# Gathering the experts of 32 more tokens, and building the expert weights from factored one-hots

## The chip, the cores and the metric

The kernel runs on one core of a Trainium2 chip. The metric is the device time of one execution in microseconds (us); three runs of the kernel before gave 1546.71 (median), from 1545.36 to 1548.38. Durations and waits below come from one profiled execution of 1544.91 us.

## The reference

One decoder layer for 512 tokens of width 1024: an input projection, differential attention and retention side by side, an output projection, then the PEER experts, then a gated input embedding and a last RMSNorm. The change is in the experts alone:

```python
qry = (m @ w_query).reshape(B, S, 8, 2, 128)
scores = jnp.einsum('bshcd,hckd->bshck', qry, sub_keys)
vals, idx = lax.top_k(scores, 16)                    # 16 of 128 keys, for each half
cand = vals[..., 0, :, None] + vals[..., 1, None, :]
cand_idx = idx[..., 0, :, None] * 128 + idx[..., 1, None, :]
top_s, top_pos = lax.top_k(cand.reshape(..., 256), 16)
expert = take_along_axis(cand_idx, top_pos)          # i * 128 + j
gates = softmax(top_s)
act = gelu(einsum('cd,ced->ce', x, u[expert])) * gates
out = einsum('ce,ced->cd', act, v[expert])
```

Each token has 8 x 16 = 128 chosen experts out of 16,384. `u` and `v` are 16,384 x 1024 in float32.

## The kernel before

The experts are computed in two ways. For the first ND = 384 tokens (three blocks of 128) all experts are computed densely and weighted with a matrix that is zero where an expert wasn't chosen. For the last 128 tokens (block 3) the chosen rows of `u` and `v` are gathered. To keep float32 precision each dense product is a sum of three matmuls of high and low parts (`wh`, `wl`, `ah`, `al`, `xh`, `xl`): ScalarE cuts the high part (L746, L755), VectorE subtracts to get the low one (L762, L764).

**Dense units.** 128 `u` units (L769, by `project` and `product3` at L85): for 128 experts i * 128 + j with the same i, 24 matmuls that stream the 384 tokens into the PSUM tile `ps`; ScalarE applies Gelu into `av` (L810). 128 `v` units (L782): 18 matmuls that add the 128 weighted experts, with the tokens as the stationary operand (three blocks of 128) and 512 columns of `v`, into the PSUM tiles `acc`. A unit's table tile of 512 KB is loaded into `wraw` three to four units ahead (RAW = 4) on SyncE's queue. The first 24 units (KEEP) keep `av` in SBUF; those of the early loop after them store it to the DRAM tile `a` and load it again.

**Gathered tokens.** GpSimd issues an indirect DMA (L848) that fetches, for each of 128 tokens, the row of one rank r out of `u` or `v` (512 KB). `sparse_step` (L853) consumes it on VectorE: for `u` a dot product with `mtok` into a column of `act` (L859), for `v` a multiply-add into `yacc` (L861). There are 256 such steps, in the list `order` (from L826). Three row buffers (ROWS) stand in `late`; six more (MORE) exist from the start of the late loop until shortly before the point END (64 units before its end), where the loads for the last stage begin. A buffer that comes free is refilled by `gather` (L836).

**Weights.** `choose(b)` (L1006) ranks the candidates of a block on VectorE; for blocks 0 to 2 a `turn` puts i, j and gate into columns by token (`it`, `jt`, `mh`, `ml`: the gate in two float16 parts). `weights_map(b, z)` (L1111) takes a RUN of 32 tokens, eight at a time: four VectorE instructions over 1024 elements (L1163 to L1166) make one-hots of j (`A`) and of i times the two gate parts (`Bh`, `Bl`), and `tail` (L1117) multiplies them on TensorE, 16 matmuls for eight tokens, into `pg`, which ScalarE copies out; the map of a RUN is written to `g_d` and read back as `gv` in quads for the `v` units (L752 multiplies it into `av`).

**Order.** Everything is issued in an order that the program works out from written costs. In the early loop (L1190) each turn is one `u` unit; it adds 4.1 to a clock `pe` (and 0.5 for a tail) and 1.25 to a clock `dve`, and then takes steps of the generator `side` (choose(3), then for each of the three blocks choose and four RUNs) for as long as `dve` is behind `pe`; each step adds 0.86 (SLOW) times the cost that it yields. After each group of eight tokens up to two gather steps are taken if a third clock, of DMA traffic, allows them (L1169). The loop ends when `side` is exhausted. What it leaves, the late loop (L1379) does: the remaining `u` units and all 128 `v` units, eight tiles of the gate weight, the remaining gather steps spread so that planned traffic per unit is level (`level`, L1376) up to the last twelve units, and the loads that the end needs (`ends`, L1353).

The lines that set the pace of the planner:

```python
clock["dve"] += 1.25                       # L1194, one u unit's wl
clock["pe"] += 4.1                         # L1201, one u unit
clock["dve"] += SLOW * c                   # L1225, c is what a step yields: 2.75 for a token group
while done[0] < n_sp and (traffic + LOAD <= level * passed or n >= total - SPARSE_END):   # L1407
```

Of the kernel before, what the change touches and what calls it, by code (L numbers as in the profile page):

```python
# [23 lines left out]
F32 = mybir.dt.float32  # L24
# [3 lines left out]
I32 = mybir.dt.int32  # L28
# [11 lines left out]
NT = 3  # L40
ND = NT * P
HEADS = 8
# [12 lines left out]
def block_kernel(ctx: ExitStack, tc, t):  # L55
# [89 lines left out]
    with pool("wa", 2, side="right") as wa, pool("sm", 2, side="right") as sm, \  # L145
# [552 lines left out]
        g_sp = late.tile([P, P], F32, name="g_sp")  # L698
        act = late.tile([P, P], F32, name="act")
        junk = late.tile([P, D], BF16, name="junk")  # L700
        nc.gpsimd.memset(yacc, 0.0)
# [34 lines left out]
        def prepare(u, low):  # L736
            kind, i = u
            w = raw.pop(u)
            if kind == "g":
                for d in range(2):  # L740
                    c = slice(d * S, (d + 1) * S)
                    scaled_split(fin["gh"][i][d], fin["gl"][:, i, c], w[:, c], gains[:, G_PLE, i:i + 1])
                return
            wh = wt.tile([P, D], F32R, name="wh", tag="wh")
            wl = wt.tile([P, D], F32R, name="wl", tag="wl")
            nc.scalar.activation(wh, w, AF.Copy)  # L746
            parts[u] = wh, wl
            if kind == "v":
                gv, av = inputs.pop(u)
                if gv is not None:  # L750
                    av3 = av.rearrange("p (z t) -> p z t", t=RUN)
                    nc.vector.tensor_tensor(av3, gv, av3, op=OP.mult)  # L752
                ah = vp[0].tile([P, ND], F32R, name="ah", tag="ah", bufs=2)
                al = vp[0].tile([P, ND], F32R, name="al", tag="al", bufs=2)
                nc.scalar.activation(ah, av, AF.Copy)  # L755
                parts[u] += ah, al
            if low is nc.gpsimd:

                nc.scalar.activation(wl, w, AF.Copy, scale=-1.0)
                nc.gpsimd.dma_start(wl.bitcast(F32), w, accum_op=OP.add)  # L760
            else:
                low.tensor_tensor(wl, w, wh.bitcast(F32), op=OP.subtract)  # L762
            if kind == "v":
                nc.vector.tensor_tensor(al, av, ah.bitcast(F32), op=OP.subtract)  # L764

# [53 lines left out]

        vp, acc, count, done_u = [], [], [0], []  # L820
        writes, spills = [], []
# [14 lines left out]
        def gather():  # L836

            while due:
                more = due.pop(0)
                if issued[0] >= n_sp or (more and not extra):  # L840
                    continue
                n = issued[0]
                issued[0] += 1
                table, r = order[n]
# [3 lines left out]
                nc.gpsimd.indirect_dma_start(out=rows[n], out_offset=None, in_=t[table],  # L848
                                             in_offset=bass.IndirectOffsetOnAxis(ap=e_sp[:, r:r + 1], axis=0))

        at_more, MORE = {}, 6

        def sparse_step():  # L853
            n = done[0]
            done[0] += 1
            table, r = order[n]
            row = rows.pop(n)
            if table == "peer_u":
                nc.vector.tensor_tensor_reduce(junk, row, mtok, 1.0, 0.0, OP.mult, OP.add, act[:, r:r + 1])  # L859
            else:  # L860
                nc.vector.scalar_tensor_tensor(yacc, row, act[:, r:r + 1], yacc, op0=OP.mult, op1=OP.add)  # L861
            due.append(at_more.pop(n))
            if table == "peer_u" and r % TOPK == TOPK - 1:
                hs = slice(r + 1 - TOPK, r + 1)
                nc.scalar.activation(act[:, hs], act[:, hs], AF.Gelu)
                nc.vector.tensor_tensor(act[:, hs], act[:, hs], g_sp[:, hs], op=OP.mult)

        with pool("wp", 2, side="right") as wpp:
# [50 lines left out]
            nc.sync.dma_start(ple_d[:, :, halves[1]], kp)  # L919
            nc.vector.tensor_tensor(mtok, mn[3], gffn, op=OP.mult)  # L920
    k_stack = ctx.enter_context(ExitStack())
    g_stack = ctx.enter_context(ExitStack())
    with pool("pk") as pk, pool("psG", 2, space=PSUM) as psG, pool("psT", space=PSUM) as psT:
# [73 lines left out]
        gsp = g_stack.enter_context(pool("gsp", side="right"))  # L997
        mh = pk.tile([P, ND], F16, name="mh")
        ml = pk.tile([P, ND], F16, name="ml")
        it = pk.tile([P, ND], BF16, name="it")  # L1000
        jt = pk.tile([P, ND], BF16, name="jt")
        later, soon = [], []
# [3 lines left out]
        def choose(b):  # L1006
# [77 lines left out]
            if b >= NT:  # L1084
                nc.vector.scalar_tensor_tensor(ij[:, 0], ij[:, 0], float(NKEY), ij[:, 1], op0=OP.mult, op1=OP.add)
                nc.vector.tensor_copy(e_sp, ij[:, 0].rearrange("p h k -> p (h k)"))
                due.extend([False] * ROWS)
                yield 0.5
                return
            turned = []  # L1090

            def turn():

                bs = slice(b * P, (b + 1) * P)
# [4 lines left out]
                nc.scalar.activation(it[:, bs], pt[:, 0], AF.Copy)  # L1099
# [11 lines left out]
        def weights_map(b, z):  # L1111
# [31 lines left out]
            def write(q0, q1):  # L1143
                nc.sync.dma_start(g_d[q0:q1, :, g].rearrange("q j x t -> j q (x t)"),
                                  gs[0][:, q0 * QUAD:q1 * QUAD].rearrange("j (q x) t -> j q (x t)", x=QUAD))

            for t0 in range(0, RUN, 8):
                while len(later) >= LATER:
# [9 lines left out]
                def per_token(x):  # L1158
                    c = b * P + z * RUN + t0
# [80 lines left out]
    def open_fin():  # L1240
# [9 lines left out]
        fin["gl"] = fp.tile([P, KC, D], F32R, name="gl", bufs=1)  # L1250
        for name in ("gate_b", "final_gain"):
            fin[name] = fp.tile([P, D], F32, name=name, bufs=1)
        fin["st"] = fp.tile([P, 8], F32, name="st", bufs=1)
# [66 lines left out]
    with pool("acc", space=PSUM) as pa:  # L1320
        vp.append(mp)
        acc += [[pa.tile([P, S], F32, name=f"acc{b}{d}") for d in range(2)] for b in range(NT)]
        V_END, total_u = 24, 0
# [54 lines left out]
        for n, u in enumerate(seq):  # L1378
# [32 lines left out]
            if 0 <= n - end_at < len(ends):  # L1411
                name, b = ends[n - end_at]
                if b is None:
                    nc.sync.dma_start(fin[name], row_src(name))
                else:
                    nc.sync.dma_start(fin[name][:, b], sources[name][:, b])
# [96 lines left out]
```

## Time and profile before

| | |
|---|---|
| median of three runs | 1546.71 us |
| profiled execution | 1544.91 us |
| its span, first to last instruction | 1543.1 us |
| TensorE busy | 1515.5 us (98%) |
| VectorE busy | 1223.0 us (79%) |
| ScalarE busy | 676.4 us (44%) |
| GpSimd busy | 384.1 us (25%) |
| moved by DMA | 401.67 MB |

The time is that of the execution; the span leaves out 1.8 us around the first and the last instruction. Busy time counts an engine as busy if any of its instructions runs, so a share is an average over stages with different limits, and a busy TensorE need not run at its peak. A line named L85 is a helper: the tile names (`ps`, `S`, `wo`) tell its callers apart.

### The profile page before, as it was taken

How to read it: one execution, taken by the hardware profiler on the slowest of the kernel's cores; microseconds unless marked ns; L12 is line 12 of the kernel's file. 1: busy time of each engine (PE TensorE's matmuls, PEld its weight loads, DVE VectorE, ACT ScalarE, POOL GpSimd, SP SyncE). 2: the span in 40 equal slices, each digit the busy share in tenths (PEclk: the TensorE clock that was granted, in tenths of full speed). 3: DMA queues.
4: the chain of work that ended last, by engine and by line, in shares of the span. 5: the costliest groups of instructions: out<-in, count | busy, mean ns of one | idle time of the engine just before them, and what ended most of it. 6: DMA issues, size and time to landing. Idle time of an engine off the chain costs nothing.

```text
span 1543.1 us, 22928 instructions
## 1 busy us (share of the span) xinstructions
PE 1515.5 (98%) x8197; PEld 1342.0 (87%) x8197; DVE 1223.0 (79%) x2529; ACT 676.4 (44%) x1075; POOL 384.1 (25%) x321
## 2 busy tenths in 40 slices
PE   8999999999999999999999999999999999999996
PEld 6787887888999999999999989898988888888885
DVE  3767555779998999898985888988888885987755
ACT  4554645444634454453434333333333333453444
POOL 1300000110023203202224555554434311422000
PEclk9999999999999999999999999999999999999999
DMA  6412335773468979887999989999999988999601
GB/s 230 148 62 80 103 107 205 215 189 110 161 205 276 299 239 306 303 287 251 308 312 372 382 315 377 343 377 393 365 355 368 348 323 314 352 377 354 243 17 41
DMA packets 163378, 401.67 MB, mean 260 GB/s; under 512 B 14687, under 2 KB 77418, under 8 KB 163136
## 3 DMA queue, kind: packets, MB, share of 16 engines
q1 hardware_dynamic: 123248, 256.06, 46.7%
q0 software_dynamic: 40016, 144.15, 27.6%
q8 instruction: 64, 1.05, 0.3%
q14 instruction: 50, 0.41, 0.1%
HBM read 350.61 MB, written 42.21 MB: 255 GB/s over the span
## 4 chain that ended last, share of the span: by engine, by line
PE 88%; DVE 7%; DMA 3%; ACT 1%; issue 1%; SPq 0%; ACTq 0%; DVEq 0%
PE ps L85 44%; PE acc L782 31%; PE S L85 2%; PE S L322 2%; PE ps L518 1%; PE pg L1123 1%; PE pg L1125 1%; PE wo L85 1%; DVE wl L762 1%; PE sc L957 1%; DMA wraw<-in_w_val_dram 1%; DMA av<-a 1%; PE po L458 1%; PE po L639 1%; DMA wraw<-in_gate_w_dram 1%
## 5 line engine op out<-in xcount | busy, mean ns | idle before, releaser
L85 PE MATMUL ps<-xh,wh 128*128 128x384 f32 (+1 forms) x1312 | 464.0, 354 | 1.6 <-ACT av L810 0.8
L85 PE MATMUL ps<-xh,wl 128*128 128x384 f32 (+1 forms) x1312 | 457.3, 349 | 3.4 <-DVE wl L762 3.4
L85 PE MATMUL ps<-xl,wh 128*128 128x384 f32 (+1 forms) x1320 | 457.9, 347 | 0.0
L762 DVE TENSOR_TENSOR wl<-wraw,wh 128x1024 fp32r<-128x1024 f32 x260 | 317.4, 1221 | 77.5 <-ACT wh L746 76.8
L746 ACT ACTIVATE wh<-wraw 128x1024 fp32r<-128x1024 f32 x272 | 286.7, 1054 | 201.2 <-PE ps L85 94.7
L848 POOL DMA_INDIRECT row<-in_peer_u_dram,e_sp x128 | 174.0, 1359 | 360.6 <-DVE yacc L861 225.4
L848 POOL DMA_INDIRECT row<-in_peer_v_dram,e_sp x128 | 169.6, 1325 | 374.2 <-DVE act L859 277.3
L85 PEld LDWEIGHTS ps<-xh,wl 128*128 128x128 f32 x1312 | 247.4, 189 | 15.7 <-DVE wl L762 4.1
L85 PEld LDWEIGHTS ps<-xh,wh 128*128 128x128 f32 x1312 | 247.9, 189 | 13.9 <-ACT av L810 1.1
L85 PEld LDWEIGHTS ps<-xl,wh 128*128 128x128 f32 x1320 | 249.2, 189 | 10.2
L782 PE MATMUL acc<-wh,ah 128*128 128x512 f32 x768 | 237.1, 390 | 0.6 <-ACT ah L755 0.6
L782 PE MATMUL acc<-wl,ah 128*128 128x512 f32 x768 | 236.8, 390 | 0.0
L782 PE MATMUL acc<-wh,al 128*128 128x512 f32 x768 | 236.7, 390 | 0.0
L782 PEld LDWEIGHTS acc<-wl,ah 128*128 128x128 f32 x768 | 144.2, 188 | 30.1
L782 PEld LDWEIGHTS acc<-wh,al 128*128 128x128 f32 x768 | 144.2, 188 | 30.0 <-DVE al L764 0.2
L782 PEld LDWEIGHTS acc<-wh,ah 128*128 128x128 f32 x768 | 144.0, 188 | 30.1 <-ACT ah L755 1.0
L861 DVE SCALAR_TENSOR_TENSOR yacc<-row,act,yacc 128x1024 f32<-128x1024 f32 x128 | 163.9, 1280 | 2.0 <-DMA row<-in_peer_v_dram,e_sp 1.8
L859 DVE CUSTOM_DVE_ANT_0 junk<-row,mtok 128x1024 bf16<-128x1024 f32 x128 | 156.0, 1219 | 1.9 <-DMA row<-in_peer_u_dram,e_sp 1.6
L755 ACT ACTIVATE ah<-av 128x384 fp32r<-128x384 f32 x104 | 54.6, 525 | 228.5 <-PE acc L782 179.3
L764 DVE TENSOR_TENSOR al<-av,ah 128x384 fp32r<-128x384 f32 x104 | 57.8, 556 | 63.0 <-ACT ah L755 62.8
L1133 ACT ACTIVATE gs<-pg 128x832 f32<-128x832 f32 x48 | 41.6, 866 | 144.8 <-PE pg L1125 144.8
L752 DVE TENSOR_TENSOR av<-gv,av 128x384 f32<-128x384 f32 x104 | 57.5, 553 | 7.4 <-DMA av<-a 6.8
(288 smaller groups left out, 1686.4 us busy)
## 6 DMA issues: line engine op xcount, KB each, us to landing
wraw<-in_u_t_dram SPq DMA_DIRECT2D x128, 512.0 KB, 5.8
wraw<-in_peer_v_dram SPq DMA_DIRECT2D x128, 512.0 KB, 6.8
gv<-g_d SPq DMA_DIRECT2D x26, 768.0 KB, 8.4
a<-av SPq DMA_DIRECT2D x72, 192.0 KB, 4.2
g_d<-gs SPq DMA_DIRECT2D x24, 576.0 KB, 7.4
av<-a SPq DMA_DIRECT2D x72, 192.0 KB, 6.1
wraw<-in_w_in_t_dram SPq DMA_DIRECT2D x16, 512.0 KB, 3.3
wraw<-in_wq_t_dram SPq DMA_DIRECT2D x16, 512.0 KB, 4.1
```

The source lines that it names most:

```text
L85: nc.tensor.matmul(out, a, b, start=first and k == 0, stop=last and k == n - 1)
L322: nc.tensor.matmul(out, *((a, b) if q_first else (b, a)), start=n == 0, stop=n == 1)
L746: nc.scalar.activation(wh, w, AF.Copy)
L752: nc.vector.tensor_tensor(av3, gv, av3, op=OP.mult)
L755: nc.scalar.activation(ah, av, AF.Copy)
L762: low.tensor_tensor(wl, w, wh.bitcast(F32), op=OP.subtract)
L764: nc.vector.tensor_tensor(al, av, ah.bitcast(F32), op=OP.subtract)
L782: nc.tensor.matmul(acc[b][d], a[:, c], bb[:, d * S:(d + 1) * S], start=f, stop=l)
L848: nc.gpsimd.indirect_dma_start(out=rows[n], out_offset=None, in_=t[table], in_offset=bass.IndirectOffsetOnAxis(ap=e_sp[:, r:r + 1], axis=0))
L859: nc.vector.tensor_tensor_reduce(junk, row, mtok, 1.0, 0.0, OP.mult, OP.add, act[:, r:r + 1])
L861: nc.vector.scalar_tensor_tensor(yacc, row, act[:, r:r + 1], yacc, op0=OP.mult, op1=OP.add)
L1133: nc.scalar.activation(gs[0][:, :, t0:t0 + 8], pgi[:, KEEP:], AF.Copy, scale=2.0 ** -15)
```

## The change

Of block 2 only the first 96 tokens stay dense: ND is 352 (11 RUNs), and the last 32 tokens of that block are gathered like block 3. For them a tile `e_x` holds the experts with partitions (q, x): 32 tokens x in each of four groups q of 32 ranks, so that one indirect DMA of 128 rows serves four ranks of each of the 32 tokens. That is 32 more steps for each table, 64 in all, with their own tokens `mtok_x`, gates `g_x`, activations `act_x` and sum `yacc_x`, listed in `order` behind the 256 of before. At the end `fold`, a matrix of ones and zeros, adds the four groups of `yacc_x` into the last 32 tokens of `acc` of block 2 by two float32 matmuls. `u` units stream 352 columns; for the `v` units `ah` and `al` lie in three rotating pairs of 384 columns whose last 32 are zeroed once.

The one-hot of i times a gate part, before one comparison and two products over 1024 elements for eight tokens, is now made of a one-hot of the high part of i (`ih`, 16 wide, times each gate part: `hh`, `hl`) and one of its rest (`il`, 8 wide: `lo`), built for 32 tokens at once; for eight tokens two products over 1024 elements give `Bh` and `Bl`. `turn` has four more small instructions that split i. A RUN now yields 1.5 + 4 x 2.05 in place of 4 x 2.75. `gate_b` and `final_gain` are loaded into `mtok_x` and `mtok` at `total - 8` rather than into tiles of their own with `ends`.

```diff
+NX = 32
+ND = NT * P - NX
+QX = P // NX
...
-                ah = vp[0].tile([P, ND], F32R, name="ah", tag="ah", bufs=2)
-                al = vp[0].tile([P, ND], F32R, name="al", tag="al", bufs=2)
-                nc.scalar.activation(ah, av, AF.Copy)
+                ah, al = pads[0]
+                pads.append(pads.pop(0))
+                nc.scalar.activation(ah[:, :ND], av, AF.Copy)
...
-        for h in range(HEADS + 1):
-            for k in range(TOPK):
-                if h < HEADS:
-                    order.append(("peer_u", h * TOPK + k))
-                if h > 0:
-                    order.append(("peer_v", (h - 1) * TOPK + k))
+        for x, n in ((0, P // TOPK), (1, NX // TOPK)):
+            for h in range(n + 1):
+                for k in range(TOPK):
+                    if h < n:
+                        order.append(("peer_u", x, h * TOPK + k))
+                    if h > 0:
+                        order.append(("peer_v", x, (h - 1) * TOPK + k))
...
+            nc.vector.tensor_tensor(mn[2], mn[2], gffn, op=OP.mult)
+            for q in range(QX):
+                nc.gpsimd.dma_start(mtok_x[q * NX:(q + 1) * NX], mn[2][P - NX:])
...
+            if b == NT - 1:
+                ef = pk.tile([P, HEADS, TOPK], F32, name="ts", tag="ts")
+                ei = pk.tile([P, P], I32, name="pos", tag="pos")
+                nc.vector.scalar_tensor_tensor(ef, ij[:, 0], float(NKEY), ij[:, 1], op0=OP.mult, op1=OP.add)
+                nc.vector.tensor_copy(ei, ef.rearrange("p h k -> p (h k)"))
+                gx = ij[:, 2].rearrange("p h k -> p (h k)")
+                for q in range(QX):
+                    for x, y in ((e_x, ei), (g_x, gx)):
+                        nc.gpsimd.dma_start(x[q * NX:(q + 1) * NX], y[P - NX:, q * NX:(q + 1) * NX])
+                yield 0.5
...
+                step8 = 1.5 * 2.0 ** 26
+                nc.vector.tensor_scalar(gb, ih, -3.5, step8, op0=OP.add, op1=OP.add)
+                nc.vector.tensor_scalar(gb, gb, -step8, None, op0=OP.add)
+                nc.vector.tensor_tensor(il, ih, gb, op=OP.subtract)
+                nc.vector.tensor_copy(ih, gb)
...
+            nc.vector.tensor_tensor(hl, io2[:, 0:P:8][:, None].to_broadcast(parts_of), per_pair(ih, P // 8), op=OP.is_equal)
+            nc.vector.tensor_tensor(lo, io2[:, 0:8][:, None].to_broadcast([P, RUN // 2, 8, 2]), per_pair(il, 8), op=OP.is_equal)
+            nc.vector.tensor_tensor(hh, hl, per_pair(mh, P // 8), op=OP.mult)
+            nc.vector.tensor_tensor(hl, hl, per_pair(ml, P // 8), op=OP.mult)
+            yield 1.5
...
-                nc.vector.tensor_tensor(Bl, io, per_token(it), op=OP.is_equal)
                 nc.vector.tensor_tensor(A, io, per_token(jt), op=OP.is_equal)
-                nc.vector.tensor_tensor(Bh, Bl, per_token(mh), op=OP.mult)
-                nc.vector.tensor_tensor(Bl, Bl, per_token(ml), op=OP.mult)
+                g4, full = slice(t0 // 2, t0 // 2 + 4), [P, 4, P // 8, 8, 2]
+                for x, y in ((Bh, hh), (Bl, hl)):
+                    nc.vector.tensor_tensor(x.rearrange("p g (h l) k -> p g h l k", l=8), y[:, g4, :, None].to_broadcast(full),
+                                            lo[:, g4, None].to_broadcast(full), op=OP.mult)
-                yield 2.75
+                yield 2.05
...
-                for z in range(P // RUN):
+                for z in range((min(ND, b * P + P) - b * P) // RUN):
...
-        ends = [("hs", b) for b in (3, 0, 1, 2)] + [("final_gain", None), ("gate_b", None)]
+        ends = [("hs", b) for b in (3, 0, 1, 2)]
...
             if n == total - 8:
                 assert done[0] == n_sp
                 add_experts(3, [yacc[:, d * S:(d + 1) * S] for d in range(2)])
+                for d in range(2):
+                    nc.tensor.matmul(acc[NT - 1][d], fold, yacc_x[0][:, d * S:(d + 1) * S], start=False, stop=False)
+                for name in ("final_gain", "gate_b"):
+                    nc.sync.dma_start(fin[name], row_src(name))
```

## Rows read from the trace of the kernel before

**Rows 1.** Page, the chain that ended last: shares by engine, then by line.

```profile
PE 88%; DVE 7%; DMA 3%; ACT 1%; issue 1%; SPq 0%; ACTq 0%; DVEq 0%
PE ps L85 44%; PE acc L782 31%; PE S L85 2%; PE S L322 2%; PE ps L518 1%; PE pg L1123 1%; PE pg L1125 1%; PE wo L85 1%; DVE wl L762 1%; PE sc L957 1%; DMA wraw<-in_w_val_dram 1%; DMA av<-a 1%; PE po L458 1%; PE po L639 1%; DMA wraw<-in_gate_w_dram 1%
```

**Rows 2.** Busy us by stage: its length, engines with instructions, granted clock, DMA share, GB/s.

```profile
261.00:368.00 107.00, 105.37 (x532) 88.28 (x531) 81.27 (x479) 50.72 (x68) 10.45 (x12) 1.00 0.67 178
368.00:430.00 62.00, 56.67 (x316) 55.61 (x314) 61.17 (x272) 33.85 (x41) 3.06 (x3) 0.97 0.39 134
430.00:826.00 396.00, 395.18 (x2767) 387.53 (x2768) 348.06 (x643) 174.00 (x265) 90.68 (x70) 1.00 0.85 282
826.00:1435.00 609.00, 608.44 (x2863) 526.37 (x2863) 511.85 (x660) 232.04 (x322) 249.84 (x184) 1.00 0.96 358
1435.00:1484.00 49.00, 49.00 (x221) 40.60 (x220) 29.64 (x47) 19.07 (x28) 0.00 (x0) 1.00 0.40 141
```

**Rows 3.** Chain in order of time: start us, us, what (xcount of instructions).

```profile
359.15 0.91 PE sc L957 x8
...
430.75 9.69 PE ps L85 x48
440.44 0.07 PE pg L1123
...
441.36 8.38 PE ps L85 x48
...
809.80 33.33 PE ps L85 x192
...
1097.64 57.16 PE acc L782 x252
```

**Rows 4.** VectorE's instructions in order of time: start us, us, instruction.

```profile
455.21 0.69 DVE L1163 TENSOR_TENSOR Bl<-io,it 128x1024 f16<-128x1024 bf16 x1
...
457.75 1.22 DVE L762 TENSOR_TENSOR wl<-wraw,wh 128x1024 fp32r<-128x1024 f32 x1
458.88 0.17 DVE L800 TENSOR_TENSOR kept<-kept,av 128x16 f32<-128x16 f32 x1
458.97 1.22 DVE L859 CUSTOM_DVE_ANT_0 junk<-row,mtok 128x1024 bf16<-128x1024 f32 x1
...
460.23 1.23 DVE L859 CUSTOM_DVE_ANT_0 junk<-row,mtok 128x1024 bf16<-128x1024 f32 x1
...
716.68 1.27 DVE L861 SCALAR_TENSOR_TENSOR yacc<-row,act,yacc 128x1024 f32<-128x1024 f32 x1
717.88 1.21 DVE L762 TENSOR_TENSOR wl<-wraw,wh 128x1024 fp32r<-128x1024 f32 x1
```

**Rows 5.** Groups by line and shape: busy us, mean ns of one, then idle before.

```profile
L762 DVE TENSOR_TENSOR wl<-wraw,wh 128x1024 fp32r<-128x1024 f32 x260 | 317.4, 1221 | 77.5 <-ACT wh L746 76.8
L764 DVE TENSOR_TENSOR al<-av,ah 128x384 fp32r<-128x384 f32 x104 | 57.8, 556 | 63.0 <-ACT ah L755 62.8
L1163 DVE TENSOR_TENSOR Bl<-io,it 128x1024 f16<-128x1024 bf16 x33 | 22.6, 686 | 0.0
L1057 DVE TENSOR_TENSOR w<-m,pairs 128x2048 bf16<-128x2048 bf16 x4 | 4.9, 1222 | 0.1
```

**Rows 6.** DMA issues: instruction and count; gathers between 430 and 820 us.

```profile
L818 SPq DMA_DIRECT2D a<-av x72: 319/320/1408, 375.2 to 827.8; - x72
...
row<-in_peer_u_dram,e_sp POOLq DMA_INDIRECT x40, 6.4
row<-in_peer_v_dram,e_sp POOLq DMA_INDIRECT x26, 6.7
...
gv<-g_d SPq DMA_DIRECT2D x26, 768.0 KB, 8.4
```

**Rows 7.** Busy us in stretches of the late loop, columns as in rows 2.

```profile
830.00:890.00 60.00, 60.00 (x306) 54.75 (x305) 50.20 (x63) 22.87 (x33) 33.43 (x23) 1.00 1.01 391
1000.00:1030.00 30.00, 30.00 (x156) 27.71 (x155) 25.54 (x33) 10.37 (x16) 17.38 (x13) 1.00 1.02 403
1030.00:1070.00 40.00, 40.00 (x178) 33.12 (x178) 37.20 (x50) 14.46 (x20) 20.38 (x15) 1.00 0.98 374
```

More of the change, by code (lines that the diff above doesn't have):

```diff
@@ L699, in block_kernel @@
         act = late.tile([P, P], F32, name="act")
+        mtok_x = late.tile([P, D], F32, name="mtok_x")
+        e_x = late.tile([P, NX], I32, name="e_x")
+        g_x = late.tile([P, NX], F32, name="g_x")
+        act_x = late.tile([P, NX], F32, name="act_x")
+        yacc_x = []
         junk = late.tile([P, D], BF16, name="junk")
@@ L763, in prepare @@
             if kind == "v":
-                nc.vector.tensor_tensor(al, av, ah.bitcast(F32), op=OP.subtract)
+                nc.vector.tensor_tensor(al[:, :ND], av, ah[:, :ND].bitcast(F32), op=OP.subtract)
         def products(u):
@@ L818, in spill @@
                 nc.sync.dma_start(*spills.pop(0))
-        vp, acc, count, done_u = [], [], [0], []
+        vp, acc, count, done_u, pads = [], [], [0], [], []
         writes, spills = [], []
@@ L843, in gather @@
                 issued[0] += 1
-                table, r = order[n]
+                table, x, r = order[n]
                 where, bufs = (extra["p"], MORE) if more else (late, ROWS)
@@ L848, in gather @@
                 nc.gpsimd.indirect_dma_start(out=rows[n], out_offset=None, in_=t[table],
-                                             in_offset=bass.IndirectOffsetOnAxis(ap=e_sp[:, r:r + 1], axis=0))
+                                             in_offset=bass.IndirectOffsetOnAxis(ap=(e_sp, e_x)[x][:, r:r + 1], axis=0))
         at_more, MORE = {}, 6
@@ L855, in sparse_step @@
             done[0] += 1
-            table, r = order[n]
+            table, x, r = order[n]
             row = rows.pop(n)
+            ac = (act, act_x)[x]
             if table == "peer_u":
-                nc.vector.tensor_tensor_reduce(junk, row, mtok, 1.0, 0.0, OP.mult, OP.add, act[:, r:r + 1])
+                nc.vector.tensor_tensor_reduce(junk, row, (mtok, mtok_x)[x], 1.0, 0.0, OP.mult, OP.add, ac[:, r:r + 1])
             else:
-                nc.vector.scalar_tensor_tensor(yacc, row, act[:, r:r + 1], yacc, op0=OP.mult, op1=OP.add)
+                y = yacc_x[0] if x else yacc
+                nc.vector.scalar_tensor_tensor(y, row, ac[:, r:r + 1], y, op0=OP.mult, op1=OP.add)
             due.append(at_more.pop(n))
@@ L864, in sparse_step @@
                 hs = slice(r + 1 - TOPK, r + 1)
-                nc.scalar.activation(act[:, hs], act[:, hs], AF.Gelu)
-                nc.vector.tensor_tensor(act[:, hs], act[:, hs], g_sp[:, hs], op=OP.mult)
+                nc.scalar.activation(ac[:, hs], ac[:, hs], AF.Gelu)
+                nc.vector.tensor_tensor(ac[:, hs], ac[:, hs], (g_sp, g_x)[x][:, hs], op=OP.mult)
         with pool("wp", 2, side="right") as wpp:
@@ L997, in block_kernel @@
         gsp = g_stack.enter_context(pool("gsp", side="right"))
[L998 to L1001, printed above, removed]
+        mh = pk.tile([P, P], F16, name="mh")
+        ml = pk.tile([P, P], F16, name="ml")
+        ih = pk.tile([P, P], BF16, name="ih")
+        il = pk.tile([P, P], BF16, name="il")
+        hot = [pk.tile([P, RUN // 2, n, 2], F16, name=f"hot{k}") for k, n in enumerate((P // 8, P // 8, 8))]
+        jt = pk.tile([P, P], BF16, name="jt")
         later, soon = [], []
@@ L1098, in turn @@
                 gb = pk.tile([P, P], F32, name="gb", tag="gb")
-                nc.scalar.activation(it[:, bs], pt[:, 0], AF.Copy)
+                nc.scalar.activation(ih[:, bs], pt[:, 0], AF.Copy)
                 nc.scalar.activation(jt[:, bs], pt[:, 1], AF.Copy)
@@ L1145, in write, with per_pair @@
                                   gs[0][:, q0 * QUAD:q1 * QUAD].rearrange("j (q x) t -> j q (x t)", x=QUAD))
+            hh, hl, lo = hot
+            parts_of = [P, RUN // 2, P // 8, 2]
+            def per_pair(x, n):
+                c = z * RUN
+                return x[:, c:c + RUN].rearrange("p (g k) -> p g k", k=2)[:, :, None, :].to_broadcast([P, RUN // 2, n, 2])
+            nc.vector.tensor_tensor(hl, io2[:, 0:P:8][:, None].to_broadcast(parts_of), per_pair(ih, P // 8), op=OP.is_equal)
[3 more added lines that the diff above has]
+            yield 1.5
             for t0 in range(0, RUN, 8):
@@ L1250, in open_fin @@
         fin["gl"] = fp.tile([P, KC, D], F32R, name="gl", bufs=1)
-        for name in ("gate_b", "final_gain"):
-            fin[name] = fp.tile([P, D], F32, name=name, bufs=1)
+        fin["gate_b"], fin["final_gain"] = mtok_x, mtok
         fin["st"] = fp.tile([P, 8], F32, name="st", bufs=1)
@@ L1321, in block_kernel @@
         vp.append(mp)
+        yacc_x.append(mp.tile([P, D], F32, name="yacc_x", bufs=1))
+        nc.gpsimd.memset(yacc_x[0], 0.0)
+        fold = mp.tile([P, P], F32, name="fold", bufs=1)
+        nc.gpsimd.memset(fold, 0.0)
+        for q in range(QX):
+            r = slice(q * NX, (q + 1) * NX)
+            nc.scalar.activation(fold[r, P - NX:], ident[r, r], AF.Copy)
+        for k in range(3):
+            pads.append([mp.tile([P, NT * P], F32R, name=f"a{z}{k}", bufs=1) for z in "hl"])
+            for x in pads[k]:
+                nc.scalar.activation(x[:, ND:], ident[:, :NX], AF.Copy, scale=0.0)
         acc += [[pa.tile([P, S], F32, name=f"acc{b}{d}") for d in range(2)] for b in range(NT)]
@@ L1412, in block_kernel @@
                 name, b = ends[n - end_at]
[L1413 to L1416, printed above, removed]
+                nc.sync.dma_start(fin[name][:, b], sources[name][:, b])
             if n == total - 8:
```

5 lines of the change are left out of this document (2 added, 3 removed).

## The prediction, made before the changed kernel ran

> **What bounds the kernel now.** I read the chain of waits first, summed by engine and line [rows 1]: TensorE holds 88% of it, the products `ps` at L85 44% and `acc` at L782 31%. So the span is a queue of matmuls, and any other engine counts only where it makes that queue wait. Next the busy times by stage [rows 2], with the edges taken from the chain in order of time [rows 3] (192 matmuls that end at 843.1 are eight `u` units, four of them of the late loop, so the early one ends at 826.5). From 368 to 430 us VectorE is busy 61.2 of 62 us and TensorE 56.7: VectorE sets the pace there (ranking of tokens, first stretch of the early loop). From 430 to 826 us TensorE is busy 395.2 of 396, VectorE 348.1. From 826 to 1435 TensorE has no gap to speak of (608.4 of 609), VectorE 511.9, and the DMA engines are at 0.96 and 358 GB/s. The last twelve units, to 1484, have light traffic (141 GB/s). The reader is to see that three resources stand close together in the late loop: whoever adds DMA and VectorE work there and takes away TensorE work must show that the order does not turn.
>
> **What a matmul costs.** A `u` unit is 24 matmuls with 384 columns, and 192 of them take 33.33 us: 173.6 ns each, 4.165 us a unit [rows 3]. The 512-column ones take 57.16 / 252 = 226.8 ns, a `v` unit (18) 4.083 us [rows 3]. The difference over 128 columns is 0.416 ns a column, so 352 columns cost 173.6 - 32 x 0.416 = 160.2 ns and a `u` unit 3.845: 0.32 us less. Over 128 units that is 41 us of TensorE. `v` units stay as they are, since `ah` and `al` are padded to 384. A `tail` (16 small matmuls) takes 441.36 - 440.44 = 0.92 us [rows 3]; 44 in place of 48 save 3.7. All TensorE work lost: some 45 us, less the fold.
>
> **What VectorE pays.** Instructions overlap, so I go from start to start [rows 4]. The four 1024-wide 16-bit ones of a token group: 457.75 - 455.21 = 2.54 us, or 0.63 each; `wl` 1.13; the dot product of a gathered row 460.23 - 458.97 = 1.26; the multiply-add into `yacc` 1.20; so 1.23 for a gather step. A 2048-wide 16-bit instruction takes 1222 ns against 686 for 1024 [rows 5], about 0.52 ns an element above a fixed part. The change makes a RUN of 32 tokens cost: `hl`, `hh`, `hl` again at 512 wide and `lo` at 256, about 0.34 + 0.40 + 0.34 + 0.20 = 1.28, and then four times three wide ones (0.62 each), 7.5; 8.76 together against 4 x 2.54 = 10.2. With 11 RUNs for 12: 96.4 for 121.9, 25 us less. That takes the new products, whose operands repeat in two directions, at the rate of the old ones, whose `mh` already repeats across 128 elements with runs of two. The other end is the rate of a 32-bit instruction of that width, 1.13: 88 x 0.5 = 44 us more. I take the first, being nearest in form. The four small instructions in each `turn` and the two in `choose(2)` are about 3 us together.
>
> **How the planner moves.** The early loop's length comes from written costs, not from the chip. An early unit brings VectorE's clock 4.1 - 1.25 = 2.85 to spend. The map costs 48 x 2.75 x 0.86 = 113.5 before and (11 x 1.5 + 44 x 2.05) x 0.86 = 91.8 after. Followed unit by unit, with the conditions of L1169 for gather steps (1.2 x 0.86 each), the loop ends after 84 units, not 96, having done 54 gather steps, not 65. The same walk gives 96 and 65 for the kernel before, and the trace has 72 stores of `a` (96 less 24 kept) and 40 + 26 gathers between 430 and 820 us [rows 6]. So the late loop gets 12 more `u` units (44 for 32), and 320 - 54 = 266 gather steps in place of 191: all 64 new ones and 11 old ones besides.
>
> **Early loop.** 368 to 430 stays: VectorE's work there (12 units) is the same. The other 72 units: TensorE 72 x 3.845 + 44 x 0.92 + 1.4 for turns = 318.7. VectorE 348.1 - 13.7 (12 `wl`) - 25 - 13.5 (11 steps) + 3 = 299. By sevens of units VectorE's sum goes over TensorE's in five places, by 0.5 to 3.1 us, 7.3 together (units 56 to 63 are the worst: 33.7 against 30.6). So 326 where 396 was: **-70**. Bounds: -77 if TensorE alone decides, -55 if VectorE's bunching costs three times what I count.
>
> **Late loop up to its last 12 units** (609 us before). TensorE: 44 x 3.845 + 116 x 4.083 = 643. VectorE: 511.9 + 75 x 1.23 + 12 x 1.13 - 7 (208 `av` and `al` instructions 32 columns shorter, by the slope from 556 ns at 384 to 1221 at 1024 [rows 5]) = 611. DMA: 609 us x 358 GB/s = 218 MB, plus 75 rows of 524 KB = 39.3, plus 12 `u_t` tiles = 6.3, less 4.7 (12 fewer `a` reads, `gv` and `a` a twelfth smaller [rows 6]) = 259 MB. What the queues can move is the disputed number. Where they are full for long, they move 391 GB/s over 60 us and 403 over 30; a stretch at share 0.98 gives 374 [rows 7]. 259 MB take 662, 643 or 692 us. I take 662, the rate of the longest full stretch: DMA is late first, `row` and `wraw` arrive late, and TensorE waits 19 us in all. **+53**; bounds +34 (TensorE alone) and +83 (374 GB/s).
>
> The Trainium skill speaks against the change here: DMA: Bandwidth & Descriptors, section Specifications, puts HBM at about 358 GB/s for one core. By that the 259 MB would need 723 us, +114. The trace disagrees for this core running alone: 391 GB/s over 60 us [rows 7].
>
> **Small things.** `fold` is two fp32 matmuls with 512 columns. Four of 128 (eight records) take 0.91 us [rows 3], so these take about 1.8 by columns; 0.45 if the width cost nothing. They wait for the last step into `yacc_x`, which the planner puts four units earlier at the latest. `gate_b` and `final_gain` are loaded at total - 8 rather than sixty units before the end; the queues are then down to 141 GB/s [rows 2] and `close` comes after all `acc` work, so nothing, or up to 6 us if they wait for a late reader of `mtok_x`. The extra product into `mn[2]` and the four copies into `mtok_x` fall into 261 to 368 us, where VectorE is busy 81 of 107. The eight copies into `e_x` and `g_x` go through GpSimd's queue ahead of gathers; at the 1.3 us that an issue there costs (90.7 us for 70 [rows 2]) they delay it about 10 us once, in a stage in which it is busy a quarter of the time. Zeroing pads and `yacc_x` comes to under 3 us beside running matmuls.
>
> **Sum.** -70 + 53 + 2 = -15. On the profiled execution's own 1544.9 us that is 1530; the median of the three runs shown is 1.8 higher, so 1532. Of the 43 us that TensorE's work loses on balance, 28 come back as waiting.
>
> **Rivals.**
> *TensorE stays the bound in the late loop* because full queues hold 403 GB/s throughout: 643 there, -70 + 34 + 2 = -34, 1513. For it: VectorE at 611 leaves room, nine row buffers hide a long backlog. Against: the demand would be 100% of the best 30 us seen. 0.22.
> *The queues do not reach the full-stretch rate over 640 us*: slower. Place: rows and `wraw` of the late loop. At 374 GB/s the loop takes 692, total +15, 1562; at the 358 that the whole stretch shows now [rows 2] it takes 723, +46, 1593. It decides from about 382 GB/s down (-70 + 2 + 68). For it: 0.96 busy at 358 already looks near full; 52 steps for 35 fall into the last 64 units, where only three row buffers are left. Against: idle gaps of 4% are visible in that 0.96, and 391 was held for 60 us. The page named above gives the upper of these two times. 0.22.
> *The broadcast products run at the slow rate*: VectorE's 299 becomes 343 in the early loop, which then takes about 350, -46 for -70; total +9, 1556. 0.06.
> *The early loop follows VectorE throughout*, as 368 to 430 does: each unit gains little, early -55, total 0, 1547. For it: the planner's unit of 4.1 now stands above TensorE's real 3.845, so it hands VectorE more than TensorE covers. Against: 20 us of slack in the sums. 0.10.
> My forecast (1515 to 1544 as its own range) has 0.40.
>
> **How the numbers follow.** A measurement of this kernel tells about 0.2%, 3 us, from no change. Faster: 0.22, 0.36 of my 0.40, 0.03 of the last rival: 0.61. Slower: 0.20 of the queue rival, 0.06, 0.03, 0.01: 0.30. The rest, 0.09, is within. Range: from the best case less some 10 us, 1502, to past the 374 GB/s case, 1572; the 358 end and mixtures stay outside with about 0.15.
>
> **What would show it.** L85 with 352 columns at 160 ns from start to start; 60 stores of `a`; first `acc` product near 770 us in place of 843; `Bh` and `Bl` at about 0.69 us; gathers x320; late loop at over 380 GB/s with DMA share about 1.0, and TensorE waiting some 10 to 30 us there, mostly behind VectorE instructions that wait for `row`, or for `wraw`. Wrong would be: TensorE without waits at the end of the late loop (first rival), `Bh` at over 1.1 us (third), TensorE gaps in the early loop of over 20 us (fourth), GB/s of the late loop under 382 with the queues full (second).

## The result and the profile after

The changed kernel took 1530.7 us (median of four runs, 1525.5 to 1534.5) beside 1546.3 us for the kernel before on the same chip: ratio 0.9895, 95% interval 0.9864 to 0.9926. The profiled execution took 1530.3 us with a span of 1528.5.

The engines' shares and the chain of waits, from the page of the changed kernel; they answer to [rows 1]:

```profile
PE 1479.6 (97%) x8137; PEld 1302.6 (85%) x8137; DVE 1264.6 (83%) x2621; ACT 673.7 (44%) x1082; POOL 498.1 (33%) x399
...
PE 72%; DMA 10%; DVE 8%; issue 6%; ACT 2%; POOL 1%; SPq 0%; DVEq 0%; ACTq 0%; POOLq 0%
```

TensorE is still the engine that is nearly always busy, but the chain now leaves it more often: 72% for 88%, and DMA at 10% for 3%. Where it leaves it is told by the stages. Columns as in [rows 2]:

```profile
265.00:372.00 107.00, 103.44 (x507) 87.06 (x508) 78.42 (x472) 47.24 (x62) 12.47 (x16) 0.98 0.69 183
372.00:435.00 63.00, 55.15 (x322) 53.39 (x320) 61.95 (x275) 33.35 (x41) 3.04 (x3) 0.95 0.40 133
435.00:761.00 326.00, 317.94 (x2415) 311.59 (x2415) 297.55 (x605) 154.18 (x246) 76.79 (x64) 1.00 0.87 286
761.00:1210.00 449.00, 449.00 (x2234) 395.73 (x2233) 429.80 (x552) 166.40 (x233) 294.81 (x207) 1.00 1.03 408
1210.00:1290.00 80.00, 80.00 (x382) 68.93 (x381) 61.40 (x89) 28.10 (x38) 26.79 (x21) 1.00 0.96 366
1290.00:1370.00 80.00, 68.89 (x313) 57.01 (x313) 65.28 (x88) 30.10 (x44) 32.86 (x24) 0.94 0.92 332
1370.00:1472.00 102.00, 102.00 (x453) 83.80 (x453) 75.13 (x105) 43.30 (x62) 21.32 (x11) 1.00 0.74 274
...
761.00:1422.00 661.00, 649.89 (x3156) 564.70 (x3155) 602.68 (x786) 249.35 (x348) 375.79 (x263) 0.99 1.00 392
```

The reader is to see two things. In the late loop the queues run at 408 GB/s for 449 us, share 1.03, and TensorE has no gap at all in that time. All of its 11 us of waiting lie in one stretch, 1290 to 1370, in which the queues move *less* (332 GB/s).

The chain in order of time, start and us, answers to [rows 3] and gives the edges of the loops; below it the lines by form, as in [rows 5], and the DMA issues, as in [rows 6]:

```profile
271.35 7.60 DMA sk<-in_sk_t_dram
279.08 1.13 PE sc L970 x8
280.21 7.09 PE ps L87 x24
...
776.76 24.50 PE acc L789 x108
801.26 15.46 PE ps L87 x96
...
1440.70 1.72 PE acc L1475 x4
...
1467.82 4.11 PE acc L789 x18
```

```profile
L769 DVE TENSOR_TENSOR wl<-wraw,wh 128x1024 fp32r<-128x1024 f32 x260 | 317.6, 1222 | 55.9 <-ACT wh L753 55.0
L771 DVE TENSOR_TENSOR al<-av,ah 128x352 fp32r<-128x352 f32 x104 | 54.2, 521 | 0.0
L1212 DVE TENSOR_TENSOR Bl<-hot,hot 128x1024 f16<-128x1024 f16 x30 | 20.8, 692 | 0.0
L1212 DVE TENSOR_TENSOR Bh<-hot,hot 128x1024 f16<-128x1024 f16 x30 | 20.7, 689 | 0.0
```

```profile
a<-av SPq DMA_DIRECT2D x60, 176.0 KB
...
row<-in_peer_u_dram,e_x POOLq DMA_INDIRECT x32
row<-in_peer_v_dram,e_x POOLq DMA_INDIRECT x32
```

Four `u` units (x96) take 15.46 us, 3.865 each, so the early loop ends 15.46 before the first `acc`, at 761.3. With 60 stores of `a` beside the 24 kept it has 84 units. The last `v` unit before the end ends at 1471.9. The first `u` product starts at 372.6 (368.0 before). That splits the span:

| part | before | after | difference |
|---|---|---|---|
| to the first `u` product | 368.0 | 372.6 | +4.6 |
| early loop | 458.5 | 388.7 | -69.8 |
| late loop | 657.7 | 710.6 | +52.9 |
| rest | 58.9 | 56.6 | -2.3 |
| span | 1543.1 | 1528.5 | -14.6 |

What happens between 1290 and 1370 is read from single instructions. The waits of all engines from 1290 to 1440 (us in total, times, longest), and then the changed kernel's instructions from 1310 to 1318 (start, us, instruction, and in brackets the idle time before it):

```profile
POOL row L856 <- DVE yacc_x L871: 55.8, 21, 7.2
ACT ah L762 <- DVE av L759: 46.8, 19, 11.1
...
DVE yacc_x L871 <- DMA row<-in_peer_v_dram,e_x: 10.0, 7, 2.8
...
PE ps L87 <- ACT av L817: 9.1, 1, 9.1
DVE junk L868 <- DMA row<-in_peer_u_dram,e_x: 8.0, 4, 2.5
```

```profile
1310.61 1.28 DVE L871 SCALAR_TENSOR_TENSOR yacc_x<-row,act_x,yacc_x 128x1024 f32<-128x1024 f32 x1 [2.81 <-DMA row<-in_peer_v_dram,e_x]
1312.17 0.94 POOL L856 DMA_INDIRECT row<-in_peer_u_dram,e_x  x1 [3.45 <-DVE yacc_x L871]
1314.31 1.23 DVE L868 CUSTOM_DVE_ANT_0 junk<-row,mtok_x 128x1024 bf16<-128x1024 f32 x1 [2.41 <-DMA row<-in_peer_u_dram,e_x]
...
1315.46 0.52 DVE L759 TENSOR_TENSOR av<-gv,av 128x352 f32<-128x352 f32 x1
...
1316.02 0.50 ACT L762 ACTIVATE ah<-av 128x352 fp32r<-128x352 f32 x1 [11.12 <-DVE av L759]
...
1316.92 0.66 PE L87 MATMUL ps<-xh,wh 128*128 128x352 f32 x1 [9.09 <-ACT av L817]
```

Read it from the bottom up. TensorE stood still for 9.09 us, since ScalarE had not yet emptied `ps` of an earlier unit (L817). ScalarE works in order and stood before `ah` for 11.12 us. `ah` needs the product `av` on VectorE, which ran at 1315.46, right behind a gather step. VectorE works in order too, and each of the two steps shown had waited for its row (2.81 and 2.41 us). A row could not come earlier: GpSimd issues it only when a step has freed a buffer. That is the ring: step, issue, landing in 6 to 8 us, step. The waits for rows make up 5.2 of ScalarE's 11.12 us; most of the rest is work that stood ahead of `av` in VectorE's order, gather steps of 1.2 to 1.3 us each and a `wl`.

A long gap costs more than its length. Behind this one 14 products take 4.08 us, 0.29 each, where 0.161 is usual: some 2 us more. The granted clock there (columns as above) is 0.50, the lower of its two levels, 1.2 GHz:

```profile
1316.90:1321.00 4.10, 4.08 (x14) 4.08 (x15) 4.10 (x7) 1.55 (x3) 1.68 (x1) 0.50 0.76 244
```

### The profile page after: what moved, and what is told of

It reads as the page before. It is cut to its first block, busy times and chain, and to the rows that moved or that the text cites. A ratio compares the mean times of both kernels' runs of the same rounds, so it can differ in the third digit from the quotient of the medians.

```text
span 1528.5 us, 22985 instructions
## 1 busy us (share of the span) xinstructions
PE 1479.6 (97%) x8137; PEld 1302.6 (85%) x8137; DVE 1264.6 (83%) x2621; ACT 673.7 (44%) x1082; POOL 498.1 (33%) x399
## 4 chain that ended last, share of the span: by engine, by line
PE 72%; DMA 10%; DVE 8%; issue 6%; ACT 2%; POOL 1%; SPq 0%; DVEq 0%; ACTq 0%; POOLq 0%
PE ps L87 32%; PE acc L789 28%; DMA wraw<-in_u_t_dram 3%; DMA row<-in_peer_u_dram,e_x 2%; PE S L87 2%; DVE wl L769 2%; DMA row<-in_peer_v_dram,e_x 2%; PE S L324 2%; PE ps L520 2%; PE wo L87 1%; POOL row L856 1%; DMA row<-in_peer_u_dram,e_sp 1%; PE sc L970 1%; DMA wraw<-in_w_val_dram 1%; PE pg L1155 1%
## 5 line engine op out<-in xcount | busy, mean ns | idle before, releaser
L87 PE MATMUL ps<-xh,wh 128*128 128x352 f32 (+1 forms) x1312 | 453.0, 345 | 12.7 <-ACT av L817 11.8
L87 PE MATMUL ps<-xh,wl 128*128 128x352 f32 (+1 forms) x1312 | 446.2, 340 | 5.6 <-DVE wl L769 5.6
L87 PE MATMUL ps<-xl,wh 128*128 128x352 f32 (+1 forms) x1320 | 446.8, 338 | 0.0
L856 POOL DMA_INDIRECT row<-in_peer_u_dram,e_sp x128 | 183.2, 1431 | 270.4 <-DVE yacc L871 116.8
L856 POOL DMA_INDIRECT row<-in_peer_v_dram,e_sp x128 | 175.3, 1370 | 164.7 <-DVE act L868 98.5
L762 ACT ACTIVATE ah<-av 128x352 fp32r<-128x352 f32 x104 | 51.9, 499 | 198.9 <-DVE av L759 169.0
L1165 ACT ACTIVATE gs<-pg 128x832 f32<-128x832 f32 x44 | 38.1, 867 | 102.6 <-PE pg L1157 99.0
L856 POOL DMA_INDIRECT row<-in_peer_v_dram,e_x x32 | 47.1, 1473 | 79.4 <-DVE yacc_x L871 38.8
L856 POOL DMA_INDIRECT row<-in_peer_u_dram,e_x x32 | 44.9, 1402 | 64.5 <-DVE act_x L868 32.1
```

The costliest lines, as they stand in the source:

```text
L87: nc.tensor.matmul(out, a, b, start=first and k == 0, stop=last and k == n - 1)
L762: nc.scalar.activation(ah[:, :ND], av, AF.Copy)
L1165: nc.scalar.activation(gs[0][:, :, t0:t0 + 8], pgi[:, KEEP:], AF.Copy, scale=2.0 ** -15)
```

## Experiments

Each kernel ran four to twelve times beside runs of the kernel before on the same chip, but not all on one chip; so kernels are compared by their ratios to the kernel before, and the changed kernel's is 0.9895 (0.9864 to 0.9926). "Late loop" is worked out as above from one profiled execution of each; a difference of some 3 us in it can be chance (see e_copies). The first question is where the 16 us that the late loop lost over TensorE's own sum come from. That sum is 44 x 3.865 + 128 x 4.083 + 2 = 694.7, and the loop took 710.6. Gaps are 11 of them, the low clock behind the longest gap some 2; the rest isn't located. One theory for the gaps is full queues, as predicted; the other is the three row buffers that are left behind END.

### e_end46: fewer gather steps on three buffers

```diff
-        W_EVERY, END = 2, total - 64
+        W_EVERY, END = 2, total - 46
```

> The point END moves from 64 to 46 units before the end; nothing else. Three-buffer theory (TensorE's 11 us of waiting between 1290 and 1370 us come from gather steps that have only three row buffers after END): nine buffers now last 18 units longer, 31 steps are left after END in place of 52 and 17 of them fall into the first 20 units; the wait goes, 1515 to 1522 us, ratio to the kernel before 0.980 to 0.985. Full-queue theory (the wait comes from the backlog that the queues built up at 409 GB/s): the traffic is the same, so 1528 to 1533.

Measured: 1524.1 us, ratio 0.9855 (0.9838 to 0.9873), between the two expectations and nearer to the first; the interval overlaps with the changed kernel's. The late loop took 702.1, 8.5 less. The stretch that held the wait, columns as above, for this kernel:

```profile
1290.00:1370.00 80.00, 74.72 (x351) 64.55 (x350) 62.52 (x83) 34.30 (x49) 19.13 (x16) 0.98 0.97 364
```

TensorE is busy 74.7 of 80 for 68.9, at a higher transfer rate and not a lower one. That speaks against full queues. Part of the gain was lost again in the early loop (393.0 for 388.7); see the end of this part.

### e_end82: more gather steps on three buffers

```diff
-        W_EVERY, END = 2, total - 64
+        W_EVERY, END = 2, total - 82
```

> END moves from 64 to 82 units before the end. Three-buffer theory: 82 steps in place of 52 fall behind END, nearly two a unit at first; three buffers turn over a row in some 3.1 us, so these 18 units cost up to 6 us in place of 4.08: 20 to 40 us slower than the changed kernel, 1550 to 1570. Full-queue theory: the same as the changed kernel, or a few us faster, since fewer gathers are in flight at a time.

Measured: 1548.9 us, ratio 1.0023 (1.0010 to 1.0035), just under what was expected of the buffers. The late loop took 727.2, 16.6 more. The wait now begins earlier, where END is; windows of this kernel:

```profile
1200.00:1290.00 90.00, 80.13 (x365) 67.69 (x364) 69.89 (x97) 26.61 (x39) 37.95 (x30) 0.94 0.91 323
1290.00:1370.00 80.00, 67.59 (x310) 57.22 (x309) 62.37 (x83) 25.40 (x37) 31.94 (x27) 0.94 0.89 319
```

In the changed kernel 1210 to 1290 had no gap; here 10 us are missing, at 323 GB/s. With 82, 64 and 46 units behind END the late loop takes 727, 711 and 702. The wait moves with END and grows with the number of steps behind it; the queues move 319 to 323 GB/s in it, far from the 408 that they reach, so full queues aren't what holds these rows up. But END moves three things at once: the point at which six buffers go, the start of the loads for the last stage, and the planned traffic. That the buffers are what counts among these is read from the ring in the single instructions above, where GpSimd waits for a step before each issue, and from e_cap1 below, which leaves END and the loads alone.

### e_copies: the four copies into mtok_x

Only the 32 rows that are needed are multiplied, straight into their place; the three copies that are left move into `choose(2)`, beside the copies of `e_x`.

```diff
-            nc.vector.tensor_tensor(mn[2], mn[2], gffn, op=OP.mult)
-            for q in range(QX):
-                nc.gpsimd.dma_start(mtok_x[q * NX:(q + 1) * NX], mn[2][P - NX:])
+            nc.vector.tensor_tensor(mtok_x[P - NX:], mn[2][P - NX:], gffn[P - NX:], op=OP.mult)
...
+                for q in range(QX - 1):
+                    nc.gpsimd.dma_start(mtok_x[q * NX:(q + 1) * NX], mtok_x[P - NX:])
```

> The tokens for the 32 gathered ones are multiplied straight into the last 32 partitions of mtok_x, and the three copies to the other groups go out in choose(2), some 250 us later; four copies at 269 us before. Collision theory (they make the first loads of the query stage late, 4.5 us on the chain): 4 to 5 us faster than the changed kernel, 1525 to 1527, first u unit near 368 us in place of 372.6. Rival (the late loads have another cause): no change, 1530.

Measured: 1527.0 us, ratio 0.9888 (0.9870 to 0.9907). The first `u` product starts at 367.7 and not at 372.6. In the profiles of all kernels here with 32 gathered tokens it starts at 371.2 to 372.6 with the early copies and at 367.7 to 369.0 without, so the delay of the query stage, some 4 us, is these copies. They start while the first loads of that stage are issued. The issues of GpSimd and SyncE in order of time (start, us) in the changed kernel, then SyncE's in e_copies:

```profile
269.38 1.98 POOL L933 DMA_DIRECT2D mtok_x<-mn  x4 [53.89 <-DVE mn L931]
...
271.35 2.96 SPq L989 DMA_DIRECT2D sk<-in_sk_t_dram  x4
```

```profile
271.02 1.80 SPq L987 DMA_DIRECT2D sk<-in_sk_t_dram  x4
```

Issuing the four `sk` loads takes 2.96 us beside the copies and 1.80 without them; TensorE then waits 2.3 to 2.6 us for `sk`, and the unit behind it takes 7.09 us (above) where 5.48 stood before, at a granted clock of 0.68 from 279 to 283 us. Whether the issuing or the transfers themselves delay `sk` isn't separated. The total gained less than the stage: the early loop is 393.7 here, 388.7 in the changed kernel, and the intervals of the two ratios overlap. That the copies cost the stage some 4 us is shown; that they cost the kernel as much is not. The late loop took 707 us here, 3 less, although the edit lies ahead of it.

### e_best: both edits

The diffs of e_end46 and e_copies together.

> Both at once: END 46 units before the end and the copies in choose(2). If both theories hold the gains add: 1511 to 1517, ratio 0.977 to 0.981. If only one holds, its own gain.

Measured: 1519.6 us, ratio 0.9840 (0.9817 to 0.9862); above the 1511 to 1517 expected; first `u` product 368.2, early loop 391.2, late loop 703.6. Only together are the two edits clear of the changed kernel: its interval (0.9864 to 0.9926) overlaps with that of each edit by itself, and not with this one. By the ratios they gain 6 us and 1 us by themselves and 8.5 together. Query stage and late loop are 11 us shorter in this profile, the early loop 2.5 longer.

### e_onehot: the one-hots alone

The kernel before with the factored one-hots; no more tokens are gathered.

> The factored one-hots alone, with their planned costs, in the kernel before: 384 dense tokens, 128 gathered, all tables as before. Theory (TensorE's queue is the bound before, and VectorE's relief is not on it): the loop ends after 88 early units in place of 96, the 8 go to the late loop, TensorE's work is the same: 1542 to 1548, ratio 0.997 to 1.002. Rival (VectorE's 25 us are part of the gain): 1530 to 1540.

Measured: 1548.2 us, ratio 1.0022 (1.0013 to 1.0031), a little slower, at the edge of what was expected. Two windows of this kernel:

```profile
372.00:435.00 63.00, 56.69 (x320) 54.87 (x320) 61.72 (x251) 35.24 (x47) 3.06 (x3) 1.00 0.42 147
...
435.00:761.00 326.00, 325.32 (x2334) 318.85 (x2333) 296.69 (x600) 148.23 (x226) 71.77 (x56) 1.00 0.84 280
```

From 435 to 761 TensorE is busy 325.3 of 326 us, so cheaper one-hots have nothing to give. Before that VectorE is full as ever (61.7 of 63), and the products of one-hots don't lie there. The planner only moves eight `u` units from the early loop into the late one (64 stores of `a` for 72).

### e_gather: the gathered tokens alone

The changed kernel with the one-hots of the kernel before and `yield 2.75`.

> The 32 gathered tokens alone, with the one-hots and the planned costs of before (four wide instructions for eight tokens). Theory (the whole gain is that u units stream 352 columns, and VectorE has room): 88 early units, VectorE some 15 us more in the early loop, four units fewer in the late one: 1526 to 1538, ratio 0.988 to 0.995, near the changed kernel's. Rival (without the cheaper one-hots VectorE sets the pace of the early loop): 1540 or more.

Measured: 1525.9 us, ratio 0.9875 (0.9860 to 0.9889). That is at least the changed kernel's gain (the intervals overlap), so it comes from the 352-column `u` units; nothing that the factored one-hots add to it can be seen. VectorE has 314 us of work from 435 to 761 in place of 298, and there is room for that: TensorE is busy 323.5 of those 326 us.

### e_nx64: what full queues would look like

```diff
-NX = 32
+NX = 64
```

> 64 tokens gathered in place of 32 (320 dense ones): u units 0.32 us shorter again, 128 gather steps added in place of 64. Queue theory (at 409 GB/s the late loop of the changed kernel is at the limit, so each further row is paid in full): about 290 MB before the last twelve units, 709 us, and a longer wait behind three buffers: 1555 to 1585. Rival (the queues have room, only the three buffers cost): TensorE's work falls another 41 us, 1500 to 1530.

Measured: 1601.7 us, ratio 1.0366 (1.0344 to 1.0387), above what was expected. Two windows of this kernel, and TensorE's waits over the whole span:

```profile
790.00:1170.00 380.00, 349.50 (x1676) 291.94 (x1675) 366.73 (x479) 121.36 (x178) 270.11 (x192) 0.98 1.03 408
1170.00:1290.00 120.00, 107.55 (x504) 92.08 (x504) 105.56 (x142) 35.70 (x53) 58.31 (x45) 0.93 0.99 381
```

```profile
PE ps L87 <- ACT av L817: 33.3, 8, 9.5
PE acc L789 <- ACT ah L762: 23.7, 18, 4.9
PE ps L87 <- DVE wl L769: 17.0, 17, 3.4
PE acc L789 <- DVE wl L769: 9.3, 10, 3.0
```

The queues run at 408 GB/s again, no faster with more to move, and here TensorE misses 30 us of 380 at that rate. The trace shows row loads on the chain at 10 to 16 us. That is what the prediction described, but it isn't shown to be the cause: VectorE is busy 366.7 of these 380 us and waits for rows only 9.4, so VectorE's own work is a rival that no run separates from the queues. In the changed kernel VectorE is as near to its end, 429.8 of 449 from 761 to 1210. A little further on one of the two would decide; in the changed kernel neither makes TensorE wait between 761 and 1290.

### e_cap1: the steps behind END spread evenly

e_best, and behind END at most one gather step a unit until the last twelve units.

```diff
+            taken = done[0]
-            while done[0] < n_sp and (traffic + LOAD <= level * passed or n >= total - SPARSE_END):
+            while done[0] < n_sp and (n < END or n >= total - SPARSE_END or done[0] == taken) and \
+                    (traffic + LOAD <= level * passed or n >= total - SPARSE_END):
```

> The version with END 46 units before the end and the late copies, and after END at most one gather step a unit. Three-buffer theory: the 6 us that TensorE still waits near 1300 us come from two steps a unit behind END; with one a unit they go, the late loop takes 695 to 699 us: 1511 to 1517. If another cause holds the rows back: 1519 as without the cap, or slower by the steps that pile up before the end.

Measured: 1516.6 us, ratio 0.9818 (0.9806 to 0.9831), the fastest by its median. The stretch, and TensorE's waits for ScalarE's `av` over the whole span (11.8 in the changed kernel), this kernel:

```profile
1290.00:1370.00 80.00, 78.73 (x375) 67.58 (x375) 63.76 (x86) 37.25 (x53) 22.38 (x16) 1.00 0.99 381
```

```profile
PE ps L87 <- ACT av L817: 4.2, 3, 1.6
```

TensorE is busy 78.7 of 80 and the late loop takes 696.6, within 2 us of TensorE's own sum. Against e_best the cap is the only edit and takes 7 us off the late loop (the intervals of the two ratios overlap); END and the loads for the end are the same. So 14 of the 16 us go when fewer steps are left on three buffers and these are spread: the gaps come from gather steps in bursts there.

### e_cap64: the spreading alone

The changed kernel with the diff of e_cap1 only, END as it was.

> The changed kernel with one edit: behind END (64 units before the end, as it stands) at most one gather step a unit, until the last twelve units. Theory (what the late loop loses is bursts of gather steps on three row buffers, each a chain of a VectorE step, a GpSimd issue and 6 to 8 us of landing, so pacing alone helps with the same 52 rows behind END): late loop 700 to 705 in place of 710.6, time 1520 to 1526, TensorE's waits behind the activations of `u` units 8 us or less in place of 11.8. Rival (the number of rows behind END decides, however they are spread, and those that are left over fall into the last twelve units): 1530 or more, with the wait moved behind 1430 us.

Measured: 1526.1 us, ratio 0.9888 (0.9870 to 0.9905), at the edge of what was expected, and by its ratio no gain over the changed kernel that is clear of noise. The late loop took 706.6: only 4 of the 16 us. The long wait is gone and short ones stand in its place, from its waits by engine:

```profile
PE acc L789 <- ACT ah L762: 8.8, 7, 2.7
...
PE ps L87 <- ACT av L817: 2.8, 2, 1.4
```

So spreading is not enough; beside e_cap1 it seems that the number of rows that have to turn over on three buffers counts as well. More buffers behind END were not tried.

### e_top: the best version without the factored one-hots

e_gather with the three edits of e_cap1.

> The gathered tokens without the factored one-hots (as in e_gather), with the three edits of e_cap1 (late copies of `mtok_x`, END 46, at most one gather step a unit behind END). Theory (the factored one-hots save VectorE time where nothing waits for it): 1512 to 1518, within 4 us of e_cap1's 1516.6 on either side; first `acc` product about 18 us later (four more `u` units in the early loop) and the late loop shorter by about as much. Rival (with the late loop at TensorE's own sum, VectorE's 25 us in the early loop now decide): 1522 or more, with the early loop over 411 us for its 88 units.

Measured: 1518.8 us, ratio 0.9842 (0.9827 to 0.9858), just above the range and 2 us from e_cap1. Its profiled span is 1514.9 us and that of e_cap1 1514.7. First `acc` product at 788.5 (12 us later than in e_cap1, 18 were expected), late loop 685.3 (11 less). The one-hots are worth 2 us by the medians and nothing by the spans even here, and the two intervals overlap: a use for them isn't shown.

What stays open: over these kernels with 84 units the early loop takes 388.6 to 393.7 us. The late copies fall into it, but e_end46 (393.0), e_end82 and e_cap64 (388.6) change nothing in its code. No run tells why.

## Why the prediction was right, and where it was not

**Early loop, -70: right.** -69.8, with 84 units and 34 + 20 = 54 gathers issued from 435 to 761, as the walk of the planner said. TensorE was busy 317.9 of those 326 us (318.7 forecast), VectorE 297.6 (299). A `u` unit was forecast at 3.845 and takes 3.865; over 128 units that is 2.6 us.

**Late loop, +53: right in size, wrong in its cause.** 392 GB/s over 661 us are 259 MB, the forecast amount; 661 us are the forecast length (662). But the step "DMA is late first, `row` and `wraw` arrive late, TensorE waits 19 us", at 391 GB/s, failed. The queues carry 408 GB/s, at which 259 MB take 635 us, less than TensorE's 643: by the queues the first rival (1513) would have come. The 391 of [rows 7] was no limit; it was a demand that the queues met. TensorE's 11 us of waits come from another place. It was named in the second rival ("only three row buffers are left"), but as one more argument on the queues' rate and without a price: behind END a row costs a ring of step, issue and landing, and VectorE, waiting in order for it, holds back the `av` products. Its price is 14 us: e_cap1, with fewer steps on that ring and these spread, reaches 696.6 where the changed kernel takes 710.6. Of the signs that the prediction named, those of its own forecast came true: over 380 GB/s, share 1.0, TensorE waiting 10 to 30 us behind VectorE instructions that wait for `row`. They couldn't tell full queues from a ring. That the 19 us of forecast waits and the 16 us lost lie close together is chance.

**A rule on bandwidth.** The Trainium skill, DMA: Bandwidth & Descriptors, section Specifications, was set aside in the prediction, and this trace disagrees with its 358 GB/s more plainly: 408 over 449 us. The Trainium skill, HBM Reference, section Specifications (TRN2), says that a core streaming alone measures well above its share; the runs here, on one core, agree with 408.

**The query stage, put at nothing: wrong by 4.6 us.** The prediction looked at VectorE's idle time there (busy 81 of 107) and not at the queues. The four copies collide with the first loads of the stage, on which TensorE waits (e_copies). That the sum still came out, -14.6 for -15, is luck: the late loop with the fold was forecast at +55 and came to +52.9, and the end came 2.3 us shorter, for which nothing was forecast.

**Broadcast products: right.** `Bh` and `Bl` take 0.69 us. But of the 25 us less on VectorE only 15 were theirs, by the prediction's own sums (11 x (10.2 - 8.76)); the other 10 are the RUN that is left out, which e_gather saves too. Measured they are fewer: VectorE is busy 1211.0 us in e_onehot and 1223.0 before, and 1264.6 in the changed kernel and 1274.3 in e_gather. These 10 to 12 us are without use that can be seen: e_onehot shows that alone they make nothing faster, and e_gather that the change does as well without them. The prediction counted them within the early loop's balance and did not ask what the change is worth without them.

**Fold and end: right.** 1.72 us for 1.8 forecast; the late loads of `gate_b` and `final_gain` cost nothing that is seen (the rest is 2.3 us shorter).

## What to carry to other kernels

A rate at which queues ran is a limit only if someone waited at it; before it goes into a sum as one, look whether the engine behind it stood still. Work that moves to the tail of a kernel is to be priced with the buffers that are left there: a row that needs a step, an issue and a landing to turn over can be bound by that ring at low transfer rates too (332 GB/s here). And an engine that works in order passes such a wait on to whatever stands behind it, so spread these steps, and do them while the buffers are many.

## What the runs showed of the hardware

- The queues of this one core carry 407 to 409 GB/s steadily: for 449 us in the changed kernel with TensorE never waiting, for 380 us in e_nx64 with TensorE waiting and more to move. That is above the 403 of [rows 7].
- Four copies of 128 KB, issued by GpSimd in 1.98 us, lengthen SyncE's issue of four small loads beside them from 1.80 to 2.96 us, and delay the end of the stage by some 4 us (4.8 from the changed kernel to e_copies).
- TensorE's granted clock falls behind its long gaps: after the one of 9.1 us it is 0.50 (1.2 GHz) for some 4 us, and the mean from 1290 to 1370 is 0.94. The gaps of e_cap64, at most 2.7 us each, leave it at 1.00 in the same stretch (busy 75.3 of 80), as in e_cap1 (78.7 of 80). A long gap thus costs more than its own length, a short one does not.
- A 16-bit product of 1024 elements whose operands both repeat, in two different directions, takes 689 to 692 ns, against 686 for the comparison of [rows 5].
